# A two-layer decoder on one core: the last turns by VectorE and transfers, and another division of labour in the opening

## The chip, the cores and the metric

One core of a Trainium2 chip. TensorE (PE) does the matrix products; VectorE (DVE), ScalarE (ACT) and GpSimd (POOL) work on tiles in SBUF (on chip, 128 partitions) and PSUM (where TensorE's sums land); SyncE (SP) does nothing but issue transfers, which GpSimd and ScalarE can also issue. Each engine runs its instructions in order. The metric is the device time of one execution in microseconds; the kernel before took 2267.51 us as a median of three runs (2267.19 to 2268.31).

## The reference

A decoder of two layers over 272 tokens (16 learned ones ahead of 256), width 2048, 16 heads of 128. Layer 0 attends with a forget gate, layer 1 by stick-breaking over keys and values that come from the residual stream; each is followed by a squared-ReLU network of width 8192.

```python
for layer in range(2):
    a = rms_norm(h, norm_attn[layer])
    if layer == 0:
        q, k, v, f = split(a @ fox_w_in)               # 2048 x (3*2048 + 16)
        cum = cumsum(log_sigmoid(f + b_f))
        o = forgetting_attention(q, k, v, cum)          # softmax(q k^T * s + cum_q - cum_k) v
        h = h + o @ fox_w_o
    else:
        k, v = split(rms_norm(h, kv_norm) @ w_kv)
        o = stick_breaking_attention(a @ sb_w_q, k, v)
        h = h + o @ sb_w_o
    h = h + square(relu(rms_norm(h, norm_mlp[layer]) @ w_up[layer])) @ w_down[layer]
return rms_norm(h, final_norm)[:, 16:]
```

All inputs and the output are 32-bit floats.

## The kernel before

**Products.** The residual stream lies in `hT` with the width on the partitions: 16 chunks of 128 x 272. Every large product runs in groups (`gemm_group`, one number `u` each, 96 in all): 512 columns of weights, four accumulators `acc`, and for each of four blocks `kb` of four chunks two tiles `raw_u_kb_hf` of 512 KB by SyncE's queue. Weights and x are split in two rounded parts, a high one by ScalarE (`whi`, L210; `x_a` and its like, L125) and the rest by VectorE (`wlo`, L211; L126), and three of the four products of parts are taken (L177). A weight part of a pair of chunks is 128x1024; VectorE reads `raw` and `whi` for it, both in SBUF.

**Order of the engines.** A scheduler places the instructions by their data. Around small work the program pins an instruction behind a numbered product of the running group (`behind(ins, issued[k])`, where `issued` lists the group's 192 products), so that an issue of a transfer or a copy falls at a chosen place. A transfer that is queued waits in its issuing engine's order.

**The opening.** The first group loads x and weights in pieces: the first eight chunks one by one, weights of the first chunk in two halves. Per chunk, ScalarE makes the high part of x, VectorE the rest. `Norm.add` squares each chunk on ScalarE (`sq_a`, L142, two buffers) and adds it to `ssq_a` on VectorE (L143); `finish` sums over partitions by a product with `mean_w` (`pms_a`, L148) and makes `rstd`, which the evictions of the second group need. `load_gates` loads the weights of the forget gate and builds `wf` and `both` (four small instructions of VectorE); 16 products with `hT` give the gate (`pf`, L341).

**Turns.** Attention needs values with tokens on the partitions, while they come with the head's width there. For the first three groups of four heads, VectorE turns 32x32 squares (`squares`, L395), `scratch` writes them to DRAM (`v_dram`, 8 transfers on GpSimd's queue), and `values_back` reads them back as whole turned tiles during the next group of products. For the last group of each layer `token_major` turns on TensorE instead, by products with the identity `ident` into PSUM (`pv`, L381), just ahead of the products `po` (L421, L623, L795) that use them; these run within the first group of the output projection. In layer 1 the corner of the scores is turned on TensorE as well (`pm`, L760), and that of the values (`pvc`, L782) for each of the four groups; in layer 0 by VectorE and transfers (`corner_turned`, `rows_turned`), but for the last group (`pvm`, L606). Near the end `to_token_major` turns the last four chunks of `hT` on TensorE (`ph`, L815) and ScalarE copies them to `h_tok`.

Of the kernel before, what the change touches and what calls it, by code (L numbers as in the profile page):

```python
# [15 lines left out]
P = 128  # L16
D = 2048
NC = D // P
M = 16
# [14 lines left out]
def yoco_kernel(ctx: ExitStack, tc: tile.TileContext, hT_in, gains, b_f, w_f, w_qkv0, w_o0, w_up, w_dn,  # L34
# [87 lines left out]
    def split_chunk(sp, gi, c):  # L122

        g = g_sb[:, gi, c:c + 1]
        nc.scalar.activation(sp.hi[:, c], hT[:, c, sp.t0:], AF.Copy, scale=g)  # L125
        nc.vector.scalar_tensor_tensor(out=sp.lo[:, c], in0=hT[:, c, sp.t0:], scalar=g,  # L126
                                       in1=sp.hi[:, c].bitcast(F32), op0=ALU.mult, op1=ALU.subtract)

    class Norm:


        def __init__(self, label, t0):
            self.label, self.t0 = label, t0
            self.acc = tmp.tile([P, T], F32, tag="ssq", bufs=1, name=f"ssq_{label}")

        def add(self, c):
# [6 lines left out]
            nc.vector.tensor_tensor(out=self.acc[:, t0:], in0=self.acc[:, t0:], in1=sq[:, t0:], op=ALU.add)  # L143
# [42 lines left out]
    def weights(u, kb, wblk, o1, load_x=None):  # L186
# [14 lines left out]
        for hf in range(2):  # L201
# [3 lines left out]
            if load_x is not None and kb == hf == 0:  # L205
                boxes[:1] = [(0, 1, 0, 256), (0, 1, 256, 512)]
# [8 lines left out]
    def gemm_group(wblk, sp, t0, evac, before={}, after={}, load_x=None):  # L215
# [7 lines left out]
        for kb in range(4):  # L223
# [14 lines left out]
            for kcs, ms in runs:  # L238
                pairs = ((0, sp.hi), (0, sp.lo), (1, sp.hi))
                if t0:  # L240
# [5 lines left out]
                wide = [(0, 0, 0), (1, 0, 1), (2, 1, 1)] if t0 and (u % 4 == 1 or u == 91) else []  # L246
                if u == 90:

                    wide = [(0, 0, 0), (0, 0, 1), (0, 2, 1)]
                for kc, m, part, x in products:  # L250
                    first, left[m] = kb == kc == 0 and left[m] == 3 * len(kcs), left[m] - 1
                    nw = n
                    if m == (0 if u == 90 else 3) and x is sp.hi and (kb, kc, part) in wide:
                        x, nw = sp.wide, n + 6
# [40 lines left out]
    norm = Norm("a0", 0)  # L295
    xa = Split("a0", 0)
    box = {}

    def load_x(chunks):
# [4 lines left out]
        for c in chunks:  # L304
            split_chunk(xa, G_A0, c)

    def first_norm(kb):
        if kb == 1:
            box["wf"] = load_gates()
# [11 lines left out]
    def load_gates():  # L321
        nc.scalar.dma_start(bf_sb, b_f)

        wf_sb = att.tile([P, NC, NC], F32, tag="v_sb", name="wf_sb")
        wf = att.tile([P, NC, 2 * NC], F32, tag="v_sb", name="wf")
        nc.scalar.dma_start(wf_sb, w_f)
        nc.vector.memset(wf[:, :, NC:], 0.0)
        nc.vector.tensor_tensor(out=wf[:, :, :NC], in0=wf_sb, in1=g_sb[:, G_A0, :].unsqueeze(2).to_broadcast([P, NC, NC]), op=ALU.mult)
        both = att.tile([P, P], F32, tag="pk", name="both")[:, :32]
        nc.vector.tensor_tensor(out=both, in0=ident[:, :32], in1=ident[:, 32:64], op=ALU.add)  # L330
        for i in (2, 3):
            nc.vector.tensor_tensor(out=both, in0=both, in1=ident[:, 32 * i:32 * i + 32], op=ALU.add)
        both = both[:, :NC]
        return wf, both

    def gate_products():
        wf, _ = box["wf"]
# [6 lines left out]
    def forget_gates(rstd):  # L344
# [4 lines left out]
        nc.tensor.matmul(pf[:NC, :T], box["wf"][1], parts, start=True, stop=True)  # L349
# [26 lines left out]
    def token_major(vT, pr, t0, label):  # L376

        pv = patt.tile([P, 2, 2, P], F32, tag="patt", name=f"pv_{label}")
        for i in range(2):
            for b in range(2):  # L380
                nc.tensor.transpose(pv[:, i, b, :], vT[:, 2 * pr + i, t0 + b * P:t0 + b * P + P], ident)  # L381
        v0 = att.tile([P, 2, 2, P], F32R, tag="v_sb", name=f"v0_{label}")
        v1 = tmp.tile([P, T], F32, tag="u2", name=f"v1_{label}")[:, :2 * P].rearrange("p (i d) -> p i d", i=2)
        split(v0, pv[:, :, 0, :])
        return v0, v1, nc.scalar.copy(v1, pv[:, :, 1, :]).ins

# [18 lines left out]
    def values_back(t, read, use, label):  # L405
        for pr in range(2):
            behind(nc.gpsimd.dma_start(t[:, pr], v_dram[pr].rearrange("c j a x -> (c j) (a x)")), read[pr])
        vs = []
        for pr in range(2):
            v0 = att.tile([P, 2, 2, P], F32R, tag="v_sb", name=f"v0_{label}_{pr}")  # L410
            v1 = tmp.tile([P, T], F32, tag="u2", name=f"v1_{label}_{pr}")[:, :2 * P].rearrange("p (i d) -> p i d", i=2)
            back = t[:, pr].rearrange("p (a b h i) -> p b h a i", a=4, b=2, h=2)
            behind(split(v0.rearrange("p x h (a i) -> p x h a i", a=4), back[:, 0]), use[pr])
            behind(nc.scalar.copy(v1.rearrange("p h (a i) -> p h a i", a=4), back[:, 1]), use[pr])
            vs.append((v0, v1))
        return vs
# [34 lines left out]
    def rows_turned(packs, dst, write, read, label):  # L451
# [5 lines left out]
        for a in range(4):  # L457
            behind(nc.gpsimd.dma_start(m_dram[:n].rearrange("k c j a x -> a j (k c) x")[a],
                                       t[32 * a:32 * a + 32].rearrange("j (m x) -> j m x", x=32)), write)
        behind(nc.gpsimd.dma_start(dst.rearrange("p (k y) -> p k y", k=n), m_dram[:n].rearrange("k c j a x -> (c j) k (a x)")), read)  # L460
# [32 lines left out]
    for g in range(4):  # L493
# [100 lines left out]
        turned = squares(vT, "s", f"0_{g}") if g < 3 else None  # L594
# [8 lines left out]
        if turned is None:  # L603
# [336 lines left out]
```

## Time and profile before

| what | value |
|---|---|
| median of three runs | 2267.51 us (2267.19 to 2268.31) |
| the profiled execution | 2266.66 us |
| its span, first to last instruction | 2264.9 us |
| granted TensorE clock | 1.000 |
| instructions in the span | 44932 |
| mean traffic with DRAM | 191 GB/s |

The span is what the profile covers; some 1.8 us of the execution lie outside it. A row of a timeline gives start and duration in us, the engine, the line, the operation, the tile written and the tiles read, their shapes, and how many instructions the row joins; in brackets stands the time the engine was idle before it and what ended that. Matmuls are pipelined: the duration of one is longer than the distance to the next, so that only distances between starts tell what one costs. An fp32 product is recorded as one or two instructions, depending on its operands.

### The profile page before, as it was taken

The numbers are of one execution on the slowest core, as the hardware profiler recorded it, in microseconds if no ns is written. First come the engines' busy times: TensorE is split into PE (matmuls) and PEld (weight loads), VectorE is DVE, ScalarE is ACT, GpSimd is POOL, SyncE is SP. The second block draws the span as 40 slices with busy tenths as digits, with TensorE's granted clock in tenths as the row PEclk, the third lists the DMA queues.
The fourth block names the chain that finished last, engine by engine and source line by source line (L and its number), as shares of the span: only waits on it lengthen the run. The fifth ranks groups of instructions, "written<-read, shape, count | busy, mean of one in ns | idle before, by whom it ended". The sixth has DMA issues, their size and how long they took to land.

```text
span 2264.9 us, 44932 instructions
## 1 busy us (share of the span) xinstructions
PE 2257.3 (100%) x18816; PEld 2249.7 (99%) x18816; DVE 1347.1 (59%) x1957; ACT 1059.2 (47%) x1444; POOL 105.2 (5%) x201
## 2 busy tenths in 40 slices
PE   9999999999999999999999999999999999999998
PEld 9999999999999999999999999999999999999998
DVE  7777666554455455455566677766555555555555
ACT  6444445443354344344444455555544543543554
POOL 1321210000000000000000011100000000000001
PEclk9999999999999999999999999999999999999999
DMA  7766655555555555555565566666656656566564
GB/s 240 241 199 193 226 184 175 182 172 181 182 173 182 177 175 184 175 184 177 169 192 183 181 215 209 210 208 187 198 187 195 202 189 197 188 193 201 186 200 140
DMA packets 127500, 432.32 MB, mean 191 GB/s; under 512 B 16145, under 2 KB 22817, under 8 KB 127297
## 3 DMA queue, kind: packets, MB, share of 16 engines
q1 hardware_dynamic: 119520, 412.59, 56.8%
q0 software_dynamic: 5456, 13.44, 1.9%
q10 hardware_dynamic: 2320, 3.43, 0.5%
q8 instruction: 147, 2.41, 0.4%
q14 instruction: 57, 0.46, 0.1%
HBM read 417.42 MB, written 11.98 MB: 190 GB/s over the span
## 4 chain that ended last, share of the span: by engine, by line
PE 99%; DMA 0%; ACT 0%; DVE 0%; issue 0%; POOL 0%; POOLq 0%; SPq 0%; ACTq 0%; DVEq 0%
PE acc L177 97%; PE po L421 1%; PE ps L421 0%; PE pz L421 0%; DMA raw<-w_qkv 0%; PE pz L742 0%; PE ps L539 0%; PE po L623 0%; PE po L795 0%; DMA hT<-hT_in 0%; ACT whi L210 0%; PE pf L341 0%; DVE wlo L211 0%; PE pv L381 0%; ACT x_a L125 0%
## 5 line engine op out<-in xcount | busy, mean ns | idle before, releaser
L211 DVE TENSOR_TENSOR wlo<-raw,whi 128x1024 fp32r<-128x1024 f32 (+1 forms) x773 | 928.0, 1216 | 702.7 <-ACT whi L210 695.4
L210 ACT ACTIVATE whi<-raw 128x1024 fp32r<-128x1024 f32 (+1 forms) x773 | 797.3, 1051 | 982.8 <-PE acc L177 946.4
L177 PE MATMUL acc<-x_m,whi 128*128 128x272 f32 (+1 forms) x4096 | 643.0, 281 | 0.0
L177 PE MATMUL acc<-x_u,whi 128*128 128x272 f32 (+1 forms) x3968 | 626.0, 281 | 0.0
L177 PEld LDWEIGHTS acc<-x_m,whi 128*128 128x128 f32 x4096 | 565.8, 188 | 0.1
L177 PEld LDWEIGHTS acc<-x_u,whi 128*128 128x128 f32 x3968 | 550.2, 188 | 0.0
L177 PE MATMUL acc<-x_m,wlo 128*128 128x272 f32 (+1 forms) x2048 | 440.7, 281 | 0.0
L177 PE MATMUL acc<-x_u,wlo 128*128 128x272 f32 (+1 forms) x1984 | 431.5, 281 | 0.0
L177 PE MATMUL acc<-x_a,whi 128*128 128x272 f32 (+1 forms) x2048 | 352.2, 285 | 0.4 <-ACT x_a L125 0.3
L177 PEld LDWEIGHTS acc<-x_m,wlo 128*128 128x128 f32 x2048 | 323.3, 188 | 0.0
L177 PEld LDWEIGHTS acc<-x_u,wlo 128*128 128x128 f32 x1984 | 315.1, 188 | 0.0
L177 PEld LDWEIGHTS acc<-x_a,whi 128*128 128x128 f32 x2048 | 300.0, 188 | 1.9 <-issue 0.9
L177 PE MATMUL acc<-x_a,wlo 128*128 128x272 f32 (+1 forms) x1024 | 252.9, 285 | 0.2 <-DVE wlo L211 0.2
L177 PE MATMUL acc<-x_kv,whi 128*128 128x272 f32 x1024 | 192.8, 288 | 0.0
L177 PEld LDWEIGHTS acc<-x_a,wlo 128*128 128x128 f32 x1024 | 175.5, 188 | 0.8 <-DVE ssq_a L143 0.4
L177 PE MATMUL acc<-x_o,whi 128*128 128x272 f32 (+1 forms) x1024 | 162.5, 282 | 0.0
L177 PEld LDWEIGHTS acc<-x_kv,whi 128*128 128x128 f32 x1024 | 160.2, 188 | 0.0
L177 PE MATMUL acc<-x_kv,wlo 128*128 128x272 f32 x512 | 147.4, 288 | 0.0
L177 PEld LDWEIGHTS acc<-x_o,whi 128*128 128x128 f32 x1024 | 141.8, 188 | 0.0
L292 DVE TENSOR_TENSOR hT<-acc,hT 128x272 f32<-128x272 f32 (+1 forms) x156 | 67.4, 432 | 75.4 <-PE acc L177 75.2
L177 PE MATMUL acc<-x_o,wlo 128*128 128x272 f32 (+1 forms) x512 | 110.4, 281 | 0.0
L177 PEld LDWEIGHTS acc<-x_kv,wlo 128*128 128x128 f32 x512 | 96.5, 188 | 0.0
(227 smaller groups left out, 1107.4 us busy)
## 6 DMA issues: line engine op xcount, KB each, us to landing
raw<-w_up SPq DMA_DIRECT2D x256, 512.0 KB, 4.3
raw<-w_dn SPq DMA_DIRECT2D x256, 512.0 KB, 4.3
raw<-w_qkv SPq DMA_DIRECT2D x92, 512.0 KB, 4.3
raw<-w_o SPq DMA_DIRECT2D x64, 512.0 KB, 4.4
raw<-w_kv SPq DMA_DIRECT2D x64, 512.0 KB, 4.5
raw<-w_q SPq DMA_DIRECT2D x32, 512.0 KB, 4.2
p_dram<-raw_p POOLq DMA_DIRECT2D x32, 96.0 KB, 3.6
raw_p<-p_dram POOLq DMA_DIRECT2D x8, 384.0 KB, 5.0
```

Of the source, the lines that this page charges most:

```text
L177: ins = nc.tensor.matmul(*args, **kw).ins
L210: on_act = nc.scalar.activation(hp, src, AF.Copy)
L211: on_dve = nc.vector.tensor_tensor(out=lp, in0=src, in1=hp.bitcast(F32), op=ALU.subtract)
L292: nc.vector.tensor_tensor(out=hT[:, c, t0:], in0=acc, in1=hT[:, c, t0:], op=ALU.add)
L421: product = nc.tensor.matmul(out, a[i], b[j], start=start and k == 0, stop=stop and k == 2)
```

## The change

It moves 31 of the transposes on TensorE to VectorE and transfers: the values of the last group of heads in both layers, the corner of the scores in layer 1 (all four groups), the corner of the values there (three of four), and the last four chunks of `hT`. The last heads' products (`pair`) are now called from inside the first group of the output projection, behind the products that `places` numbers, and the values' transfers go partly by SyncE's queue. In the opening VectorE makes both parts of chunk 0's x, the weights of chunk 1 are split in halves, the products of chunk 0 go part by part, `wf` and `both` are built at the start, and the 15 adds of the first norm run on GpSimd. Three extra-wide products (262 columns for 256) go, and three others move from group 90 to 61.

```diff
-    def split_chunk(sp, gi, c):
+    def split_chunk(sp, gi, c, on_dve=False):
         g = g_sb[:, gi, c:c + 1]
-        nc.scalar.activation(sp.hi[:, c], hT[:, c, sp.t0:], AF.Copy, scale=g)
+        if on_dve:
+            nc.vector.tensor_scalar(sp.hi[:, c], hT[:, c, sp.t0:], g, None, op0=ALU.mult)
+        else:
+            nc.scalar.activation(sp.hi[:, c], hT[:, c, sp.t0:], AF.Copy, scale=g)
...
-            nc.vector.tensor_tensor(out=self.acc[:, t0:], in0=self.acc[:, t0:], in1=sq[:, t0:], op=ALU.add)
+            self.engine.tensor_tensor(out=self.acc[:, t0:], in0=self.acc[:, t0:], in1=sq[:, t0:], op=ALU.add)
...
-                boxes[:1] = [(0, 1, 0, 256), (0, 1, 256, 512)]
+                boxes = [(o, 1, c, c + 256) for o in range(2) for c in (0, 256)]
...
-                if t0:
+                if t0 or (load_x is not None and kb == 0 and kcs == [0]):
                     products = [(kc, m, *pair) for pair in pairs for kc in kcs for m in ms]
...
-                wide = [(0, 0, 0), (1, 0, 1), (2, 1, 1)] if t0 and (u % 4 == 1 or u == 91) else []
-                if u == 90:
-                    wide = [(0, 0, 0), (0, 0, 1), (0, 2, 1)]
+                wide = [(0, 0, 0), (1, 0, 1), (2, 1, 1)] if t0 and u % 4 == 1 else []
+                if u == 61:
+                    wide = wide + [(3, 0, 0), (3, 0, 1), (3, 2, 1)]
                 for kc, m, part, x in products:
+                    if len(issued) in between:
+                        between[len(issued)]()
...
-    norm = Norm("a0", 0)
+    norm = Norm("a0", 0, nc.gpsimd)
...
+    box["wf"] = gate_tiles()
...
-            split_chunk(xa, G_A0, c)
+            split_chunk(xa, G_A0, c, c == 0)
...
-    def token_major(vT, pr, t0, label):
-        pv = patt.tile([P, 2, 2, P], F32, tag="patt", name=f"pv_{label}")
-        for i in range(2):
-            for b in range(2):
-                nc.tensor.transpose(pv[:, i, b, :], vT[:, 2 * pr + i, t0 + b * P:t0 + b * P + P], ident)
...
-    def scratch(t, products):
+    def scratch(t, products, queues=(nc.gpsimd, nc.gpsimd)):
...
-                ins = nc.gpsimd.dma_start(v_dram[pr].rearrange("c j a x -> a j c x")[a], y[32 * a:32 * a + 32])
+                ins = queues[pr].dma_start(v_dram[pr].rearrange("c j a x -> a j c x")[a], y[32 * a:32 * a + 32])
...
+    def values_read(t, pr, read, queue=nc.gpsimd):
+        behind(queue.dma_start(t[:, pr], v_dram[pr].rearrange("c j a x -> (c j) (a x)")), read)
...
-        turned = squares(vT, "s", f"0_{g}") if g < 3 else None
+        turned = squares(vT, "s", f"0_{g}")
+        if g == 3:
+            scratch(turned, (issued[-20], issued[-1]), (nc.gpsimd, nc.sync))
...
+    def last_heads(turned, reads, uses, places, label, pair, first=None):
+        def back(pr):
+            def run():
+                if first is not None and pr == 0:
+                    box["small"] = first()
+                pair(pr, values_back(turned, pr, issued[uses[pr]], label))
+            return run
+        def read(pr):
+            return lambda: values_read(turned, pr, issued[reads[pr]], nc.sync)
+        return {**{reads[pr] + 1: read(pr) for pr in range(2)}, **{places[pr]: back(pr) for pr in range(2)}}
+
+    box["last"] = last_heads(turned, (32, 60), (70, 108), (96, 122), "0_3", pair)
...
-        pm = patt.tile([P, 512], F32, tag="patt", name=f"pm1_{g}")
-        placed_behind(nc.tensor.transpose(pm[:, 0:P], corners(z[:, :, P:144], z[:, :, 400:416], f"sm1_{g}"), ident), product)
+        pmq = corner_turned(corners(z[:, :, P:144], z[:, :, 400:416], f"sm1_{g}"), f"1_{g}")
...
-        turned = squares(vT, "pp", f"1_{g}") if g < 3 else None
+        turned = squares(vT, "pp", f"1_{g}")
         if g < 3:
             scratch(turned, issued[-2:])
+        else:
+            scratch(turned, (issued[-20], issued[-1]), (nc.gpsimd, nc.sync))
...
+            if g < 3:
+                rows_turned([vc], vc_sb, issued[24], issued[84], f"1_{g}", nc.sync)
             else:
...
+                nc.tensor.transpose(pv[:, :P], vc, ident)
+                nc.scalar.copy(vc_sb, pv[:, :P])
...
+    box["last"] = last_heads(turned, (36, 66), (80, 116), (104, 132), "1_3", pair1, corner1)
...
     def to_token_major():
-        for b in range(2):
-            ph = patt.tile([P, 512], F32, tag="patt", name=f"ph_{b}")
-            for i in range(4):
-                nc.tensor.transpose(ph[:, i * P:(i + 1) * P], hT[:, 12 + i, M + b * P:M + (b + 1) * P], ident)
-            nc.scalar.copy(h_tok[:, b, :], ph)
+        t = squares(hT[:, 12:, M:], "pp", "h")
+        scratch(t, issued[-2:])
+        return t
+
+    def tokens_back(t):
+        for pr in range(2):
+            behind(nc.gpsimd.dma_start(t[:, pr], v_dram[pr].rearrange("c j a x -> (c j) (a x)")), issued[40 + 8 * pr])
+            back = t[:, pr].rearrange("p (a b h i) -> p b h a i", a=4, b=2, h=2)
+            for b in range(2):
+                y = h_tok[:, b, 2 * P * pr:2 * P * pr + 2 * P].rearrange("p (h a i) -> p h a i", h=2, a=4)
+                behind(nc.gpsimd.tensor_copy(y, back[:, b]), issued[80 + 8 * pr])
```

`gate_tiles` holds the allocation of `wf_sb` and `wf`, the memset of `wf` and the three sums of `both` that stood in `load_gates`.

How the instructions move. VectorE in the opening, from the second chunk's weight part to the third block's, before: the weight parts are `wlo`, the x parts `x_a`, and between them stand the norm's adds (`ssq_a`) and the gate's tiles (`wf`, `both`).

```order
L211 TENSOR_TENSOR wlo_1_1_276<-raw_1_1_252,whi_1_1_275 128x512
L327 MEMSET wf 128x16x16
L330 TENSOR_TENSOR both<-ident 128x32
L143 TENSOR_TENSOR ssq_a_138<-ssq_a_138,sq_a_4_291 128x272
L332 TENSOR_TENSOR both<-both,ident 128x32
L143 TENSOR_TENSOR ssq_a_138<-ssq_a_138,sq_a_5_294 128x272
L126 SCALAR_TENSOR_TENSOR x_a_139<-hT,g_sb,x_a_139 128x272
L332 TENSOR_TENSOR both<-both,ident 128x32
L126 SCALAR_TENSOR_TENSOR x_a_139<-hT,g_sb,x_a_139 128x272
L211 TENSOR_TENSOR wlo_2_0_366<-raw_2_0_351,whi_2_0_365 128x2x512
```

The same stretch of VectorE now:

```order
L214 TENSOR_TENSOR wlo_1_1_285<-raw_1_1_261,whi_1_1_284 128x512
L129 SCALAR_TENSOR_TENSOR x_a_139<-hT,g_sb,x_a_139 128x272
L214 TENSOR_TENSOR wlo_1_1_285<-raw_1_1_261,whi_1_1_284 128x512
L129 SCALAR_TENSOR_TENSOR x_a_139<-hT,g_sb,x_a_139 128x272 x2
L214 TENSOR_TENSOR wlo_2_0_368<-raw_2_0_353,whi_2_0_367 128x2x512
```

Nothing but parts is left there; the adds stand one after the other on GpSimd, behind its masks.

TensorE where the norm's sum is taken (`pms_a`), before: it stands among the products of the second accumulator of the second group.

```order
L177 MATMUL acc_1_580<-x_a_139,whi_0_0_587 128x272 x2
L177 MATMUL acc_1_580<-x_a_139,wlo_0_0_588 128x272
L177 MATMUL acc_1_580<-x_a_139,whi_0_1_591 128x272 x2
L177 MATMUL acc_1_580<-x_a_139,wlo_0_1_592 128x272
L148 MATMUL pms_a_536<-ssq_a_138,mean_w 128x272
```

And now:

```order
L180 MATMUL acc_3_165<-x_a_139,wlo_3_1_454 128x272
L347 MATMUL pf<-hT,wf 32x272 x3
L180 MATMUL acc_0_581<-x_a_139,whi_0_0_589 128x272 x2
L151 MATMUL pms_a_538<-ssq_a_138,mean_w 128x272
L180 MATMUL acc_0_581<-x_a_139,wlo_0_0_590 128x272
```

It has moved up to behind the group's second product (it was behind the 22nd), and three of the last four gate products stand right before that group.

SyncE at the hand-over from the last heads of layer 0 to the output projection, now (`w_o` are the projection's weights); before, the weight transfers followed each other with nothing between:

```order
L202 DMA raw_2_1_4208<-w_o 128x1024
L202 DMA raw_3_0_4301<-w_o 128x1024
L397 DMA v_dram_157<-turned_3_4050 32x4x128 x4
L202 DMA raw_3_1_4302<-w_o 128x1024
L401 DMA turned_3_4050<-v_dram_156 128x512
L401 DMA turned_3_4050<-v_dram_157 128x512
L202 DMA raw_0_0_4387<-w_o 128x1024
```

The second pair's four writes and both reads now stand between weight transfers; the first pair's writes go by GpSimd's queue.

More of the change, by code (lines that the diff above doesn't have):

```diff
@@ L628, in yoco_kernel, with pair @@
-        if g == 3:
-            outputs()
-    def out_proj(w, ao, t0, gi, label, before={}):
+        def pair(pr, v, g=g, pps=pps, own=own):
+            p0, p1 = in_order(*pps[pr])
+            v0, v1 = v
+            po = patt.tile([P, 2, 256], F32, tag="patt", name=f"po0_{g}_{pr}")
+            for i in range(2):
+                weighted(po, v0, p0, i)
+                nc.tensor.matmul(po[:, i, P:], v1[:, i, :], p1[:, i], start=False, stop=i == 1)
+            ends = po.rearrange("p i (c q) -> p (i c) q", c=2)[:, :, P - M:]
+            nc.vector.tensor_tensor(out=ends, in0=ends, in1=own[:, 4 * pr:4 * pr + 4], op=ALU.add)
+            put_split(ao, 4 * g + 2 * pr, 2, M, S, po)
@@ new lines, in outputs @@
+        def outputs(g=g, pps=pps, turned=turned, vm=vm, vc=vc, vm_sb=vm_sb, small_outputs=small_outputs, pair=pair):
+            behind(split_probabilities(*pps[1]), issued[60])
+            scratch(turned, issued[20:60:20])
+            for pr in range(2):
+                values_read(turned, pr, issued[100 + 10 * pr])
+            vs = [values_back(turned, pr, issued[160 + 10 * pr], f"0_{g}") for pr in range(2)]
+            rows_turned([vm, vc], vm_sb, issued[112], issued[130], f"0_{g}")
+            small_outputs()
+            for pr in range(2):
+                pair(pr, vs[pr])
```

152 lines of the change are left out of this document (66 added, 86 removed).

## The prediction

> **What bounds the kernel now.** I read the page's busy times first, then the chain of waits, then the waits of TensorE alone.
>
> ```profile
> PE 2257.3 (100%) x18816; PEld 2249.7 (99%) x18816; DVE 1347.1 (59%) x1957; ACT 1059.2 (47%) x1444; POOL 105.2 (5%) x201
> PE 99%; DMA 0%; ACT 0%; DVE 0%; issue 0%; POOL 0%; POOLq 0%; SPq 0%; ACTq 0%; DVEq 0%
> PE pr_fin L177 <- DVE fin L852: 0.8, 1, 0.8
> PE acc L177 <- ACT x_a L125: 0.3, 1, 0.3
> PE acc L177 <- DVE wlo L211: 0.2, 1, 0.2
> ```
>
> TensorE (PE) is busy for 2257.3 of the span of 2264.9 us, the chain is PE for 99%, and once it has begun it waits for 1.3 us in all (the columns are total, times, longest), of which the change touches the last two rows, 0.5 us. So there are two ways to move the end: take work off TensorE (the turns), or change how well the opening feeds it. VectorE (DVE, 59%) and ScalarE (ACT, 47%) have room as a mean over the span; the opening is where they have none.
>
> **The turns.** 31 transposes leave TensorE: 16 into `pv`, 8 into `ph`, 4 into `pm`, 3 of 4 into `pvc`. The timeline of TensorE shows each kind beside its neighbours (start, duration):
>
> ```profile
> 2101.52 1.04 PE L815 MATMUL ph<-ident,hT 128*128 128x128 f32 x8
> 2102.31 0.83 PE L177 MATMUL acc<-x_m,whi 128*128 128x262 f32 x5
> ...
> 321.87 0.60 PE L381 MATMUL pv<-ident,vT 128*128 128x128 f32 x4
> 322.23 0.49 PE L177 MATMUL acc<-x_o,whi 128*128 128x272 f32 x2
> ...
> 325.51 0.38 PE L381 MATMUL pv<-ident,vT 128*128 128x128 f32 x2
> 325.65 0.37 PE L421 MATMUL po<-p,v 128*128 128x256 f32 x1
> 325.85 0.38 PE L381 MATMUL pv<-ident,vT 128*128 128x128 f32 x2
> ...
> 1471.67 1.03 PE L381 MATMUL pv<-ident,vT 128*128 128x128 f32 x8
> 1472.57 0.60 PE L177 MATMUL acc<-x_o,whi 128*128 128x256 f32 x3
> ...
> 1307.34 0.27 PE L760 MATMUL pm<-ident,pk_sm 128*128 128x128 f32 x1
> 1307.37 0.49 PE L177 MATMUL acc<-x_kv,whi 128*128 128x272 f32 x2
> ...
> L381 PE MATMUL pv<-ident,vT x16: 271/272/273, 321.9 to 1472.4; 128*128 128x128 f32 x16
> ```
>
> A transpose lasts 0.272 us, but the next instruction starts long before it ends, so what it costs is the distance to that start. `ph`: 2102.31 - 2101.52 = 0.79 us for 8. `pv` in layer 0: 0.36 for 4, then 0.14 for 2, twice. In layer 1: 0.90 for 8 with the one `pvc` behind them. A lone `pm`: 0.03; four of them and two `pvc` more, 0.18. Together 0.79 + 0.36 + 0.28 + 0.90 + 0.18 = 2.5 us, the low end. The products beside them gain too: the lone `po` at 325.65 holds 0.20 us where its neighbours of the same shape need some 0.12. The high end is 31 times the pitch of a whole product, 31 x 0.12 = 3.7. I take **-3.2**, since most transposes stand in blocks with a change of operand at both ends. The block of gate products is split once more, one such change: **+0.1**. The three extra-wide products fewer have 6 columns each; nothing.
>
> [...]
>
> What takes the turns over has no one waiting: SyncE only issues, VectorE has 41% of its time idle, and the last turn's values (`h_tok`) are wanted some 150 us later. The exception is the last group of heads in each layer, where `pv` was turned on the spot and now goes to DRAM and back.
>
> ```profile
> 314.00 0.44 DVE L503 TENSOR_TENSOR vT<-acc,rstd_a 128x272 f32<-128x272 f32 x1 [1.04 <-PE acc L177]
> 317.07 0.33 SPq L199 DMA_DIRECT2D raw<-w_o  x1
> v_dram<-turned POOLq DMA_DIRECT2D x48, 64.0 KB, 3.8
> turned<-v_dram POOLq DMA_DIRECT2D x12, 256.0 KB, 5.3
> raw_p<-p_dram SPq DMA_DIRECT2D x8, 384.0 KB, 3.4
> ```
>
> The last of the four value tiles is there at 314.44. Behind it VectorE has a weight part of 1.2 us and the turns of the second pair, so SyncE can write these from about 316.5, in four issues of some 0.4 us; then comes the weight transfer that was at 317.07 (now near 318.2), then the read of the first pair at 318.6. That pair is turned two evictions, some 3 us, earlier; GpSimd writes it from 313, four issues of 0.55 and 3.8 to landing, 319.0. The read takes 3.4 to 5.3, ScalarE's and VectorE's halves 0.9: 323.3 to 325.2. The first `po` stands two products ahead of 325.51, at 325.3, less the 0.36 of the `pv` before it, 324.9: between 1.6 us of cover and a stall of 0.3. The second pair lands at 318.1 + 3.8, is read after it and ready at 326.2 to 328.1, and its `po` comes some 3 us after the first. Layer 1 has the same order of steps. I take **+0.3** for both layers, bounds 0 and 2 x 1.9 (a read by the slower row where I count on the faster one). Behind the reads on SyncE wait the next weights, 1 to 3 us later than before; a stall there is not in the sum and belongs to the fourth rival.
>
> **The opening.** Taking chunk 0's x to VectorE and chunk 1's weights in halves can save only what TensorE idles there:
>
> ```profile
> 6.55 0.41 PE L177 MATMUL acc<-x_a,wlo 128*128 128x272 f32 x2
> 7.04 1.27 PE L177 MATMUL acc<-x_a,whi 128*128 128x272 f32 x8
> 6.35 0.63 ACT L210 ACTIVATE whi<-raw 128x512 fp32r<-128x512 f32 x1 [0.38 <-DMA raw<-w_qkv]
> 4.26 0.42 ACT L210 ACTIVATE whi<-raw 128x256 fp32r<-128x256 f32 x1 [2.17 <-DMA raw<-w_qkv]
> ```
>
> Two products of 0.12 end at 6.80, the next start at 7.04, bound by the split of 512 columns that starts at 6.35 when its weights land. With 256 columns (0.42 instead of 0.63) it is there 0.2 earlier: **-0.2**. An earlier start of the first product (0.3 waited) is worth no more, since that landing comes next.
>
> The adds of the first norm are the part that can go wrong. The trace has no 128x272 add on GpSimd (POOL), but it has adds and copies of GpSimd beside VectorE:
>
> ```profile
> 2250.75 1.62 POOL L839 TENSOR_TENSOR ob<-h_tok,g_tok 128x256 f32<-128x256 f32 x2 [170.46 <-DVE h_tok L838]
> 2250.97 0.80 DVE L844 CUSTOM_DVE_ANT_0 sq_tok<-h_tok 128x256 f32<-128x256 f32 x1
> ...
> 40.31 0.29 POOL L432 COPY pk_qm<-qT 128x128 f32<-128x128 f32 x1 [34.05 <-DVE qT L499]
> ...
> 186.28 2.29 POOL L432 COPY pk_qm<-qT 128x128 f32<-128x128 f32 x1 [9.69 <-DVE qT L499]
> 186.06 2.35 DVE L211 TENSOR_TENSOR wlo<-raw,whi 128x1024 fp32r<-128x1024 f32 x2
> ...
> L432 POOL COPY pk_vm<-vT 128x128 f32<-128x128 f32 x4 | 4.4, 1088 | 3.9 <-DVE vT L503 3.9
> L874 POOL TENSOR_TENSOR ob<-hT,pr_sb 128x256 f32<-128x256 f32 x4 | 2.9, 735 | 4.3 <-ACT pr_sb L870 4.3
> ```
>
> The same copy takes 0.29 us alone and 2.29 when two weight parts of VectorE run back to back over it (mean 1088 ns in the group beside them). The other way round, VectorE's 128x256 operation of 2250.97 ends at 2251.77, and GpSimd's second add, which ends at 2252.37, fits in the 0.60 us after it. [...]
>
> ```profile
> 10.10 0.99 DVE L143 TENSOR_TENSOR ssq_a<-ssq_a,sq_a 128x272 f32<-128x272 f32 x2
> ...
> 15.50 0.27 DVE L327 MEMSET wf<- 128x256 f32 x1
> 16.63 0.49 DVE L126 SCALAR_TENSOR_TENSOR x_a<-hT,g_sb,x_a 128x272 fp32r<-128x272 f32 x1
> 17.56 1.22 DVE L211 TENSOR_TENSOR wlo<-raw,whi 128x1024 fp32r<-128x1024 f32 x1
> ...
> 18.83 0.39 PE L177 MATMUL acc<-x_a,wlo 128*128 128x272 f32 x1 [0.17 <-DVE wlo L211]
> 34.17 0.41 PE L177 MATMUL acc<-x_a,whi 128*128 128x272 f32 x2
> 34.91 0.62 PE L148 MATMUL pms_a<-ssq_a,mean_w 128*128 128x272 f32 x2
> ```
>
> Ahead of the weight part of 17.56, for which TensorE waits at 18.83, VectorE loses two adds (0.99), one more by the same row (0.4), and at 15.50 to 16.63 the memset, sums and two adds (1.13): 2.5 us. Against it stand up to five turns of GpSimd of 0.60 x 272/256 = 0.64 us: 3.2. Net **+0.7** there. If GpSimd took nothing from VectorE, the wait itself would go, 0.2 us in the table: the low end is -0.2. The ten later adds cost 10 x (0.64 - 0.36) = 2.8 more if nothing covers them, which is the high end; I count none of it, as VectorE is busy for 59% of the span and makes up a delay once the x is split.
>
> The norm's sum (`pms_a`) is the second place. It stood behind 22 products of the second group and now behind 2: six products take 34.91 - 34.17 = 0.74, so TensorE reaches it 20 x 0.123 = 2.5 earlier, at 32.4, or 32.9 with the +0.7 and -0.2. GpSimd's add alone is 735 ns x 272/256 = 0.78; with the mean wait of the copy (1.09 - 0.29 = 0.80) it is 1.58, and 15 of them from 10.1 end at 33.8: a stall of 0.9, none when the last ones run with VectorE idle. I take **+0.6**. The squares of ScalarE have two buffers, so a late add holds ScalarE too, and the weight parts behind the square.
>
> **The sum**: -3.2 + 0.1 + 0.3 - 0.2 + 0.7 + 0.6 = -1.7 us. The profiled execution took 2266.66 us, its span 2264.9; the median of the runs is 2267.51, 0.85 above. The span should come to 2263.2, and the median to **2265.8**.
>
> **Rivals.**
> A transpose costs its duration (0.11): 31 x 0.272 = 8.4 instead of 3.2 gives -6.9, 2260.6. Against it stand all the rows above in which the next product starts after 0.03 to 0.10 us; for it, that the changes of operand are seen at few places. [...]
> GpSimd takes nothing that counts (0.27): the turns, -0.2 and -0.2 at the waits, 2267.51 - 3.2 + 0.1 - 0.4 = 2264.0. For it: the lone 0.29; against it: the copies of 1 to 2 us.
> GpSimd's chain comes late (0.13, the other side): when each add waits as the copy of 186.28 did, 15 x 2.29 from 10.1 ends at 44.5, 11.6 us after TensorE is at `pms_a`: -2.3 + 11.6 = +9.3, 2276.8. It decides for slower than 0.2% once the stall passes 6.8 us, an add of (32.9 + 6.8 - 10.1) / 15 = 1.97 us; the mean row stands at 1.58.
> The values of the last heads come late in both layers (0.05): 2 x 1.9 in place of 0.3, 2269.3. For it: the waits in order on SyncE; against it: SyncE's own reads of 3.4.
>
> **How the numbers follow.** My forecast has 0.44, its own range 2264.1 to 2268.3. What a measurement of this kernel can tell from no change is about 0.2%, 4.5 us: below 2263.0 or above 2272.0. Faster: the first rival (0.11), a fifth of the second (0.06) and 0.01 of mine, 0.18. Slower: 0.11 of the third, 0.02 of the fourth, 0.01 of mine, 0.14. The rest, 0.68, lies within. The range 2262.4 to 2271.0 leaves out most of the first and of the third rival.
>
> **What would show it.** Right: no transposes of `ph`, `pm`, `pv` on TensorE and some 3 us less between unmoved places on either side of each; GpSimd's adds of more than 1 us while weight parts run; a wait of TensorE on `wlo` near 19 us and one on `ssq_a` near 33. Wrong: adds of 0.8 us with weight parts still at 1.22, or a wait on `v` near 325 and 1478, or ScalarE's squares idle for `sq_a` for several us in a row.

## The result

The changed kernel took 2271.11 us (median of 20 runs, 2267.31 to 2274.4), the kernel before 2267.98 in as many (2266.97 to 2270.19): a ratio of 1.0014 (95% interval 1.0008 to 1.0020), slower by some 3 us. It also spreads more, 7.1 us against 3.2. The profiled execution took 2272.27 us, its span 2270.6.

Of the page after, the busy times and the chain:

```profile
PE 2258.0 (99%) x18785; PEld 2249.5 (99%) x18785; DVE 1356.1 (60%) x1975; ACT 1057.1 (47%) x1439; POOL 132.0 (6%) x246
PE 96%; DMA 2%; DVE 1%; issue 1%; ACT 0%; SPq 0%; POOL 0%; POOLq 0%; ACTq 0%; DVEq 0%
```

TensorE has 31 instructions fewer and is busy for 0.7 us more: what left it came back as slower instructions (below), and the chain now holds 2% of transfers. Its waits after (total, times, longest):

```profile
PE po L414 <- ACT v L378: 3.1, 1, 3.1
PE pvc L806 <- DMA vc_sb<-m_dram: 1.9, 2, 1.5
PE idle L61 <- DVE mean_w L57: 1.1, 1, 1.1
PE pr_fin L180 <- DVE fin L881: 0.8, 1, 0.8
```

The first two are new, and both belong to turned values of layer 1. The other two stood there before, with the same 1.1 and 0.8 us. How the difference builds up is seen from the first product of each group in the two traces (start in the changed kernel less start in the kernel before; then the difference of two such numbers over a stretch):

| stretch | difference, us |
|---|---|
| opening, to the second group | +1.29 |
| layer 0's hand-over, first group of its projection | -0.88 |
| layer 1's keys and values | +1.62 |
| layer 1's hand-over, first group of its projection | +4.14 |
| the turn of `hT` near the end, two groups | -0.92 |
| everything else, up to the last group's first product | +0.0 |
| behind it, to the end of the span | +0.4 |

Of the last row, 0.3 us show as well in the run below that has nothing of the change but the adds on GpSimd, so the row is not put down to the turns.

Layer 1's hand-over on SyncE's queue after (start, duration, what is issued):

```profile
1472.77 0.34 SPq L473 DMA_DIRECT2D raw_p<-p_dram  x1
1473.21 0.66 SPq L202 DMA_DIRECT2D raw<-w_o  x1
1474.06 2.32 SPq L397 DMA_DIRECT2D v_dram<-turned  x4
1476.42 0.46 SPq L202 DMA_DIRECT2D raw<-w_o  x1
1479.48 0.83 SPq L401 DMA_DIRECT2D turned<-v_dram  x2
```

and the engines around it, GpSimd, ScalarE and TensorE:

```profile
1469.25 2.20 POOL L397 DMA_DIRECT2D v_dram<-turned  x4 [0.49 <-DVE turned L390]
1483.33 0.42 ACT L378 ACTIVATE v<-turned 128x256 fp32r<-128x256 f32 x1 [3.53 <-DMA turned<-v_dram]
1483.80 0.51 PE L414 MATMUL po<-p,v 128*128 128x256 f32 x2 [3.10 <-ACT v L378]
```

GpSimd had issued the first pair's writes by 1471.45, and they had landed by 1474.8. Their read, the second in the last row, goes out at 1479.99: ahead of it on SyncE stand the read of the probabilities (which waits for its own write), a weight transfer, the second pair's four writes, another weight transfer, and the second pair's read, which the scheduler put first and which waits until those four writes have landed. TensorE stands still from 1480.7 to 1483.8.

That is 3.1 of the 5.0 us lost there (4.14, and some 0.9 that the eight transposes had cost by the rows before). The windows of TensorE behind the wait show the rest (busy, granted clock, share and rate of the transfers):

```profile
1483.80:1485.00 1.20, 1.20 (x11) 1.00 0.87 236
1485.00:1486.00 1.00, 1.00 (x9) 0.63 0.86 332
1486.00:1487.00 1.00, 1.00 (x6) 0.50 0.89 356
1487.00:1488.00 1.00, 1.00 (x7) 0.50 0.88 307
1488.00:1489.00 1.00, 1.00 (x8) 0.67 0.93 320
1489.00:1490.00 1.00, 1.00 (x11) 1.00 0.58 234
```

The granted clock is half for 0.74 + 1 + 1 + 0.66 = 3.4 us (a window's shortfall from 1.00, divided by 0.5), which costs 1.7 us of products; it sets in 1.5 us after TensorE is busy again.

The corners of the values in layer 1, third group, on SyncE's queue, and the product on TensorE that uses them:

```profile
1422.05 2.20 SPq L451 DMA_DIRECT2D m_dram<-vt  x4
1424.35 0.39 SPq L202 DMA_DIRECT2D raw<-w_kv  x1
1430.49 0.34 SPq L453 DMA_DIRECT2D vc_sb<-m_dram  x1
1433.84 0.46 PE L806 MATMUL pvc<-pm_sb,vc_sb 128*128 128x128 f32 x2 [1.54 <-DMA vc_sb<-m_dram]
```

The last write is issued by 1424.25; the read goes out 6.2 us later, when all four have landed, and TensorE waits 1.54 us for what it brings.

### The profile page after: what moved, and what is told of

Read it like the earlier page. It is cut to its first block, busy times and chain, and to the rows that moved or that the text cites. A ratio compares the mean times of both kernels' runs of the same rounds, so it can differ in the third digit from the quotient of the medians.

```text
span 2270.6 us, 45002 instructions
## 1 busy us (share of the span) xinstructions
PE 2258.0 (99%) x18785; PEld 2249.5 (99%) x18785; DVE 1356.1 (60%) x1975; ACT 1057.1 (47%) x1439; POOL 132.0 (6%) x246
## 4 chain that ended last, share of the span: by engine, by line
PE 96%; DMA 2%; DVE 1%; issue 1%; ACT 0%; SPq 0%; POOL 0%; POOLq 0%; ACTq 0%; DVEq 0%
PE acc L180 94%; DMA m_dram<-vt 1%; PE po L414 0%; DMA vc_sb<-m_dram 0%; PE ps L414 0%; PE pz L414 0%; DMA raw<-w_qkv 0%; DVE wlo L214 0%; ACT whi L213 0%; PE pz L753 0%; PE ps L532 0%; PE po L808 0%; PE po L611 0%; DMA v_dram<-turned 0%; DMA turned<-v_dram 0%
## 5 line engine op out<-in xcount | busy, mean ns | idle before, releaser
L180 PE MATMUL acc<-x_o,wlo 128*128 128x272 f32 (+2 forms) x512 | 111.7, 284 | 0.0
```

What stands on the lines that cost most here:

```text
L180: ins = nc.tensor.matmul(*args, **kw).ins
```

## The experiments

Each time is the median of its runs, with its ratio to the kernel before on the same chip. The stretches are taken from the one profile of each run, as in the table above.

**The order of the two reads.** Only in layer 1 does it change anything: there the second pair's read is now pinned behind the first's.

```diff
-        behind(queue.dma_start(t[:, pr], v_dram[pr]...), read)
+        ins = queue.dma_start(t[:, pr], v_dram[pr]...)
+        behind(ins, read)
+        if pr and "read0" in box:
+            behind(ins, box.pop("read0").ins)
...
```

> The changed kernel with one thing altered: on SyncE the read of the first pair's turned values goes ahead of the read of the second pair's in layer 1 (in the changed kernel it stands behind it, and the second pair's read waits for the second pair's writes to land). Theory A, the order on SyncE's queue makes the 3.1 us wait of TensorE ahead of po in layer 1: the wait falls below 0.5 us, the granted clock stays at 1.00 after it, the stretch from the first to the second group of layer 1's output projection goes from 4.1 us longer than in the kernel before to about 1 us shorter, and the whole comes to about 2266 (ratio to before 0.999 to 1.000). Rival B, the transfers are simply that slow and the order does not matter: a wait of 2.5 us or more stays and the ratio stays near 1.0014.

2269.93 us, ratio 1.0007 (0.9999 to 1.0016). SyncE and TensorE:

```profile
1477.35 2.29 SPq L401 DMA_DIRECT2D turned<-v_dram  x2
1482.63 0.50 PE L418 MATMUL po<-p,v 128*128 128x256 f32 x2 [2.02 <-ACT v L378]
```

The first pair's read goes out at 1477.35 instead of 1479.99, but the wait only falls to 2.0: this read took 4.8 us to land instead of 3.3, and TensorE comes to `po` three products earlier. The clock stayed at 1.00, and the stretch is at +1.65. Neither theory holds as it stands, and one profile settles little: where the hand-over is not edited and `po` stands where it does in the changed kernel, the wait is 3.1, 2.7, 2.4 and 0.8 us in the profiles of this set. From the group's first product to the landing of the first pair's values it is 13.6 us here, and with the order of the changed kernel 14.4 to 15.1 in six profiles and 12.7 in a seventh (the next run). So the order seems to be a part of it, of about 1 us.

**The corners on GpSimd's queue.**

```diff
-                rows_turned([vc], vc_sb, issued[24], issued[84], f"1_{g}", nc.sync)
+                rows_turned([vc], vc_sb, issued[24], issued[84], f"1_{g}")
```

> The changed kernel with the transfers of the turned corner of the values in layer 1 (m_dram, vc_sb, first three groups) on GpSimd's queue instead of SyncE's. Theory A, these transfers wait in SyncE's queue among 512 KB weight transfers: the two waits of TensorE on vc_sb (0.4 and 1.5 us) go, the stretch of layer 1's key and value groups goes from 1.7 us longer than before to about 0.3 shorter, and the total falls by some 2 us (ratio about 1.0005). Rival B, turning by transfers takes that long on any queue: waits of over 1 us in sum stay.

2267.88 us, ratio 1.0003 (0.9993 to 1.0012). The waits on `vc_sb` are gone, and layer 1's keys and values take 0.80 us less than in the kernel before. With the corners on SyncE this stretch was +1.62, +1.28, +0.60, +0.51, -0.20 and between -0.66 and -0.82 in the profiles of the other runs here: the transfers are late in some executions and not in others, one source of the wider spread.

The outcome is theory A's, but its reason is not shown. The corners are no sooner back by GpSimd's queue: from the last write's issue to the read's it is 4.3 to 5.8 us there (three groups) and 3.8 to 6.6 on SyncE's (nine profiles), and in the third group the corner lands at 1435.57 here and at 1433.70 in the changed kernel. What moved is the product that waits for it: it stands behind the 178th product of its group instead of the 144th, at 1437.44 instead of 1433.84. The scheduler placed it anew with the other queue. Corners on SyncE with the later place were not run.

Nor is the lower total the corners' alone. In this profile the hand-over, which was not edited, lost less too (+1.28):

```profile
PE po L414 <- ACT v L378: 0.8, 1, 0.8
```

Here SyncE reads the probabilities back 2.7 us after the group's first product instead of 4.5, and all behind it on the queue goes out earlier.

**The norm's adds back on VectorE.**

```diff
-    norm = Norm("a0", 0, nc.gpsimd)
+    norm = Norm("a0", 0)
```

> The changed kernel with the 15 adds of the first norm back on VectorE; the rest of the new opening stays. Theory A, GpSimd and VectorE take turns at SBUF and the adds on GpSimd hold VectorE's weight and x parts: VectorE's x parts after 11 us take 0.49 again instead of up to 1.0, the second group starts about 0.4 us earlier than in the kernel before instead of 1.25 later, total lower by 1.5 us (ratio about 1.0007). Rival B, the opening's loss comes from the chunk-by-part order and the splits in halves: the second group still starts 1.0 us or more later than before.

2269.28 us, ratio 1.0006 (0.9997 to 1.0014); the profile is of the slowest run, 2271.89. The second group starts 0.10 us before that of the kernel before, instead of 1.25 after it. The groups of the opening in the changed kernel, on GpSimd and then VectorE (count, then busy us and mean ns):

```profile
L146 POOL TENSOR_TENSOR ssq_a<-ssq_a,sq_a 128x272 f32<-128x272 f32 x15 | 16.6, 1107 | 10.7 <-ACT sq_a L145 10.0
```

```profile
L214 DVE TENSOR_TENSOR wlo<-raw,whi 128x1024 fp32r<-128x1024 f32 x7 | 10.6, 1541 | 0.6 <-ACT whi L213 0.6
L129 DVE SCALAR_TENSOR_TENSOR x_a<-hT,g_sb,x_a 128x272 fp32r<-128x272 f32 x13 | 9.7, 771 | 0.7 <-ACT x_a L128 0.7
```

The same two groups of VectorE in the kernel before:

```profile
L211 DVE TENSOR_TENSOR wlo<-raw,whi 128x1024 fp32r<-128x1024 f32 x7 | 8.4, 1218 | 0.5 <-ACT whi L210 0.5
L126 DVE SCALAR_TENSOR_TENSOR x_a<-hT,g_sb,x_a 128x272 fp32r<-128x272 f32 x14 | 6.8, 495 | 0.0
```

Beside GpSimd's adds (1107 ns against 440 on VectorE) a weight part takes 1541 ns instead of 1218 and an x part 771 instead of 495. That the two engines take turns at SBUF, as theory A has it, no run shows.

**The adds on GpSimd alone**, in the kernel before, and **the old opening** in the changed kernel:

```diff
-            nc.vector.tensor_tensor(out=self.acc[:, t0:], in0=self.acc[:, t0:], in1=sq[:, t0:], op=ALU.add)
+            self.engine.tensor_tensor(out=self.acc[:, t0:], in0=self.acc[:, t0:], in1=sq[:, t0:], op=ALU.add)
```

```diff
-    norm = Norm("a0", 0, nc.gpsimd)
+    norm = Norm("a0", 0)
...
-            split_chunk(xa, G_A0, c, c == 0)
+            split_chunk(xa, G_A0, c)
...
-                boxes = [(o, 1, c, c + 256) for o in range(2) for c in (0, 256)]
+                boxes[:1] = [(0, 1, 0, 256), (0, 1, 256, 512)]
...
-                if t0 or (load_x is not None and kb == 0 and kcs == [0]):
+                if t0:
```

> The kernel before with one part of the change: the 15 adds of the first norm on GpSimd, nothing else. Theory A, GpSimd and VectorE take turns at SBUF: the second group starts 1.0 to 2.0 us later than in the kernel before, GpSimd's adds take over 1 us on average, VectorE's x parts beside them up to 1.0 instead of 0.49 (ratio 1.0005 to 1.0009). Rival B, GpSimd's adds cost VectorE nothing and free it of 15 adds: the second group starts at the same time or up to 0.4 earlier (ratio 0.9998 to 1.0000).

> The changed kernel with the old opening (adds on VectorE, chunk 0's x by ScalarE, chunk 1's weights whole, products of chunk 0 in the old order; the gate's tiles are still built at the start); the turns stay changed. Theory A, of the opening only the adds on GpSimd cost anything and the rest brings nothing: the second group starts within 0.4 us of the kernel before, as with the adds alone put back. Rival B, the other parts of the new opening cost or gain more than 0.5 us of their own. The hand-over of layer 1 and its corners keep their waits, so the ratio is near 1.0006 in both cases; the segments tell.

The adds alone: 2269.6 us, ratio 1.0010 (1.0001 to 1.0019), the second group 2.1 us later, and another 0.5 up to the sixth group. The old opening: 2268.92, ratio 1.0005 (0.9996 to 1.0014), the second group 0.22 later. So far both follow theory A: the adds cost, the rest of the new opening is worth nothing that shows. Over the whole set, from the thirteenth product to the second group TensorE needs 25.1, 25.2, 25.6 and 26.0 us where VectorE adds, 25.3 in the kernel before, and 25.9 to 27.0 (eight profiles) in the changed opening with GpSimd: 1.1 us more in the mean.

Most of that is not the slower parts, which is all that theory A names. With the adds on GpSimd (nine profiles) the last four gate products stand on TensorE in two blocks, one and three; with the adds on VectorE (five profiles, the kernel before among them) they stand in one. The block before with the product behind it, and the two blocks of the changed kernel:

```profile
26.66 0.67 PE L341 MATMUL pf<-hT,wf 128*32 128x272 f32 x8
27.26 0.40 PE L177 MATMUL acc<-x_a,wlo 128*128 128x272 f32 x1
```

```profile
27.25 0.65 PE L347 MATMUL pf<-hT,wf 128*32 128x272 f32 x2
27.83 0.39 PE L180 MATMUL acc<-x_a,wlo 128*128 128x272 f32 x1
32.98 0.66 PE L347 MATMUL pf<-hT,wf 128*32 128x272 f32 x6
33.57 0.52 PE L180 MATMUL acc<-x_a,whi 128*128 128x272 f32 x2
```

From the first gate product to the product behind the block it is 0.60 us for four of them, 0.58 for one and 0.59 for three (two records each): the block has a price, its length hardly. The second block costs 0.7 us in the changed kernel, 0.75 in the mean of the eight. That leaves some 0.3 us in the mean for the slower parts; in the profile of the changed kernel they cost TensorE nothing, in the run with the adds alone 1.2.

**Layer 1's last heads**, three ways: the first pair's products 16 products later (the second pair's 4); the first pair's read on GpSimd's queue; the turn by TensorE, as before.

```diff
-    box["last"] = last_heads(turned, (36, 66), (80, 116), (104, 132), "1_3", pair1, corner1)
+    box["last"] = last_heads(turned, (36, 66), (80, 116), (120, 136), "1_3", pair1, corner1)
```

```diff
-            return lambda: values_read(turned, pr, issued[reads[pr]], nc.sync)
+            return lambda: values_read(turned, pr, issued[reads[pr]], queues[pr])
...
-    box["last"] = last_heads(turned, (36, 66), (80, 116), (104, 132), "1_3", pair1, corner1)
+    box["last"] = last_heads(turned, (36, 66), (80, 116), (104, 132), "1_3", pair1, corner1, (nc.gpsimd, nc.sync))
```

```diff
-        turned = squares(vT, "pp", f"1_{g}")
+        turned = squares(vT, "pp", f"1_{g}") if g < 3 else None
...
-    xm, norm_m = out_proj(w_o1, ao, M, G_M1, "m1", box.pop("last"))
+    xm, norm_m = out_proj(w_o1, ao, M, G_M1, "m1", {}, {1: tensor1})
```

(`tensor1` calls `token_major` for both pairs and `pair1` on what it returns.)

> The changed kernel with the last heads' products of layer 1 placed 16 products later (120 and 136 instead of 104 and 132). Theory A, the granted clock falls to half only after a wait of TensorE of some 3 us: the wait shrinks by 16 x 0.113 = 1.8 to about 1.3 us and the slow stretch of 3 us goes with it, so the stretch to the next group gains 1.8 and some 2.3 more, 4 us in all (ratio about 0.9997). Rival B, the clock falls after any wait there, or for another reason: 1.8 us gained, and the clock still shows 0.5 for about 3 us (ratio about 1.0006).

> The changed kernel with the read of the first pair's turned values in layer 1 on GpSimd's queue, where nothing stands behind the first pair's writes; SyncE keeps the second pair. Theory A, the wait ahead of po comes from what stands before this read on SyncE (the second pair's writes, a weight transfer, the second pair's read): the read is issued near 1475.7 by the span of the changed kernel instead of 1480.0, and even with GpSimd's slower landing of some 5 us the wait falls from 3.1 to below 1.0 us, with no slow clock behind it; ratio about 1.0000. Rival B, the traffic of weights at this place makes any read late: wait of 2 us or more.

> The changed kernel with the last heads of layer 1 turned by TensorE as in the kernel before; everything else stays changed. Theory A, this hand-over alone is where the change loses its gain: the stretch to the projection's second group takes the time it takes in the kernel before (within 0.3 us) instead of 4.1 more, and the total falls by some 3 to 4 us below the changed kernel's (ratio 0.9997 to 1.0002), with less spread among runs. Rival B, the loss is spread over other places: the ratio stays above 1.0008.

Later products: 2273.16 us, ratio 1.0022 (1.0012 to 1.0033), where theory A had 0.9997; against the changed kernel's 1.0014 (1.0008 to 1.0020) the difference is not clear of the intervals. The profile is of the fastest run (2270.00). In it the wait on the values is 1.3 as expected and the clock stays at 1.00, but two new waits stand behind it:

```profile
PE po L414 <- ACT v L378: 1.3, 1, 1.3
PE acc L180 <- DVE x_o L458: 1.2, 1, 1.2
PE pvc L806 <- ACT vc_sb L794: 1.1, 1, 1.1
```

The projection needs these heads' outputs (`x_o`) in its last block, and their halves on ScalarE and VectorE no longer fit ahead of it. Neither of the two places is free: at the earlier one the values come too late for the products, at the later one the products come too late for the projection. The read on GpSimd's queue: 2267.8, ratio 1.0001 (0.9992 to 1.0010); no wait on values is left (they land 11.3 us after the group's first product), the stretch is at +1.05, all of it a wait of 1.3 us on `x_o`. Theory A holds here. The turn by TensorE: 2267.27, ratio 1.0000 (0.9991 to 1.0009), the stretch at +0.03, and the runs lie within 1.9 us. Theory A of the last: the hand-over of layer 1 alone accounts for some 3 us of the median.

**The clock.** The first products of these heads 16 products earlier and ahead of all that follows, so that the wait grows; and the same with 36 products of a constant ahead of them.

```diff
-    box["last"] = last_heads(turned, (36, 66), (80, 116), (104, 132), "1_3", pair1, corner1)
+    box["last"] = last_heads(turned, (36, 66), (80, 116), (88, 132), "1_3", pair1, corner1)
```

```diff
+            if pr == 0 and g == 3:
+                filler = patt.tile([P, 512], F32, tag="patt", name="filler")
+                for _ in range(36):
+                    nc.tensor.matmul(filler[:, :P], mean_w, mean_w, start=True, stop=True)
```

> The changed kernel with the last heads' first products of layer 1 put 16 products earlier and ahead of all that follows, so that TensorE's wait there grows to some 5 us. Theory A, a wait of TensorE longer than about 3 us halves the granted clock for a while after it: windows behind the wait show 0.50 for about 3 us. Rival B, the slow stretch in the changed kernel came from something else (traffic, the instructions there): no slow clock, or one that also shows without a wait. Total near or above the changed kernel's (ratio 1.0015 to 1.0025).

> The same as the run with the earlier place, but TensorE fills the wait with 36 products of a constant (some 4.2 us). Theory A: the values come at the same time, the wait that is left is under 2 us, the clock stays at 1.00 behind it, and the next group starts 1.5 to 2.5 us earlier than without the filler. Rival B: the clock shows 0.50 here too, and the next group starts no earlier.

Bare: 2274.28 us, ratio 1.0030 (1.0018 to 1.0042); filled: 2276.34, ratio 1.0037 (1.0023 to 1.0051). The windows of TensorE in the bare run:

```profile
1480.00:1482.00 2.00, 0.00 (x0) 0.58 0.87 274
1482.00:1484.00 2.00, 1.33 (x6) 0.50 0.89 283
1484.00:1485.00 1.00, 1.00 (x7) 0.50 0.94 377
1485.00:1486.00 1.00, 1.00 (x6) 0.50 0.74 283
1486.00:1487.00 1.00, 1.00 (x7) 0.50 0.88 240
1487.00:1488.00 1.00, 1.00 (x10) 0.93 0.34 113
```

in the filled one:

```profile
1484.00:1485.00 1.00, 1.00 (x12) 1.00 0.92 348
1485.00:1486.00 1.00, 1.00 (x11) 1.00 0.81 324
1486.00:1487.00 1.00, 1.00 (x11) 1.00 0.40 164
```

and the filler's row in its timeline (36 products, two records each):

```profile
1476.70 8.20 PE L806 MATMUL filler<-mean_w 128*128 128x128 f32 x72
```

With a wait of 5.0 us the clock is half for 1.7 + 2 + 3 + 0.1 = 6.8 us, from 1480.3 on, while TensorE still waits; with the wait filled it is never below 1.00 there. That is theory A as to the clock. The filler was mis-sized: one such product holds 0.22 us, not 0.12, so it ran 2.9 us past the values and the next group started 1.9 us later, not earlier.

Half clock came with the waits of 2.7 us (3.4 us of it, in the run with the old opening), 3.1 us (3.4, in the changed kernel) and 5.0 us (6.8, in the bare run). Behind waits of 1.3 us (the later products), 1.5 (the third corner in the changed kernel), 2.0 (the order of the reads) and 2.4 (the adds on VectorE) the clock stayed at 1.00. The 2.7 is less than the some 3 us of theory A. Whether the length of a wait alone decides is not shown, as a single profile stands for each of these.

**The repairs together**: corners on GpSimd's queue and adds on VectorE, with layer 1's last heads either read on GpSimd's queue or turned by TensorE (the edits above).

> Three repairs at once: the first pair's read in layer 1 on GpSimd's queue, the turned corner of the values in layer 1 on GpSimd's queue, the first norm's adds on VectorE. If the losses are these three and add up, by segments against the kernel before: opening -0.1, layer 0's hand-over -0.9, layer 1's corners -0.7, its hand-over between -0.9 and 0, the end -0.9; in sum -2.6 to -3.5 us, ratio 0.9985 to 0.9989. Rival: the transfers on GpSimd's queue collide, and the waits come back under other names; ratio above 0.9995.

> The repairs with layer 1's last heads turned by TensorE as before, its corners of the values on GpSimd's queue, and the adds on VectorE. If the segments add up: opening 0 to +0.6, layer 0 -0.9, layer 1's corners -0.7, its hand-over 0, the end -0.9: -1.9 to -2.5 us, ratio 0.9989 to 0.9992, with waits of TensorE on values or corners gone. Rival: ratio above 0.9996.

By GpSimd's queue 2265.44 us, ratio 0.9990 (0.9981 to 0.9999), just short of what was expected, the opening at +0.8 instead of -0.1; by TensorE 2264.65, ratio 0.9984 (0.9976 to 0.9993), better than expected. Both are faster than either kernel. One at a time, corners, adds and the turn by TensorE lowered the ratio from 1.0014 by 0.0011, 0.0008 and 0.0014, 0.0033 in sum; together they lower it by 0.0030. So by the medians, too, these three places hold the loss, each figure to about 0.001. In the second no wait is left but those of the kernel before at both ends:

```profile
PE idle L61 <- DVE mean_w L57: 1.1, 1, 1.1
PE pr_fin L180 <- DVE fin L900: 0.8, 1, 0.8
```

Its stretches: opening +0.3, layer 0 -0.88, layer 1's keys and values -0.80, its hand-over +0.03, the end -0.92; with 0.4 up to the sixth group some -2 us in the profile, as expected.

## Why the prediction was wrong, step by step

- **The turns, -3.2: right.** Where nothing waited for what took their place, 23 transposes gave 0.88 + 0.80 + 0.92 = 2.6 us, and the eight of layer 1's last heads stood for some 0.9 more by the rows before, 3.5 together. The distance between starts was the price (2.6 us for 23, 0.11 each), not the duration (0.272); the rival by the duration falls.
- **The hand-over, "Layer 1 has the same order of steps. I take +0.3 for both layers": the step that failed.** Layer 0 went as worked out (no wait, -0.88). Layer 1 has another order: SyncE also carries the probabilities there, whose read waits for its write, and the scheduler had put the second pair's read first. It cost 5.0 us in the profile where 0.15 was counted: 3.1 of waiting and 1.7 of half clock, which the prediction did not know of. With the turn back on TensorE the loss is gone (+0.03), and with the first pair's read off SyncE no wait on values is left. How the 3.1 divide between the probabilities and the order of the two reads is not settled. The fourth rival had this mechanism with a price of 3.8 for two layers and a chance of 0.05.
- **"What takes the turns over has no one waiting": wrong for the corners of the values in layer 1.** Their four writes and the read on SyncE were given no price; they cost up to 2.4 us in a profile (+1.62 against -0.80). The product that uses them stands too early for such a round trip; that the queue is to blame is not shown.
- **The opening, -0.2 + 0.7 + 0.6 = +1.1: near in size by luck**, 1.29 in the profile and 1.1 to 1.7 in the eight with this opening. VectorE's parts are slower beside GpSimd's adds (1541 ns for 1218, 771 for 495). The +0.7 counts five turns of GpSimd of 0.64 us against VectorE, and no run shows such turns: in their place the runs show the slower parts, which cost TensorE some 0.3 us in the mean. In the profile, 0.7 us is the split block of gate products, for which the sum has **+0.1**, and another 0.7 the first nine products, which stand some 0.23 us apart instead of 0.12. They end at 7.28 us. What slows them is not shown; how many are so slow varies from run to run (one in the kernel before, at 5.14). TensorE did not wait for `ssq_a` (+0.6), nor longer for the weight part near 19 us than before (+0.7); and with the first products at full pace the pause of the -0.2 was still there (0.42 us between two products near 7 us, with the adds on VectorE).

By the profile it is -3.5 for the turns, +1.3 for the opening, +5.0 for the hand-over and +2.4 for the corners, +5.2 in sum; the groups' starts differ by 5.25 at the end. The median lies at +3.1, as the waits of layer 1 vary.

## What to carry to other kernels

A turn that goes through DRAM must be followed instruction by instruction through the queue that issues it, in each place where it is used: here the first pair's values lay in DRAM at 1474.8 and their read went out at 1479.99, behind all that stood ahead of it on SyncE, where the second pair's read alone held the queue from 1476.88 to 1479.48, until its writes had landed. Where TensorE is the bound, a wait of 3.1 us cost 4.8 here, because the clock fell to half behind it for 3.4 us; it did so behind one of 2.7 too, and not behind four of 1.3 to 2.4. Before a repair is put down to a queue, look whether the product that waited still stands in its old place. Adds moved to GpSimd were not free (1107 ns each instead of 440, and VectorE's weight parts beside them 1541 instead of 1218), and products on TensorE moved with them: the last four gate products, split into two blocks, were paid twice (0.58 and 0.59 us, for 0.60 in one block).

## What was not expected

Besides the clock: in two profiles (adds on VectorE; the filled wait) TensorE's 256-column products have a pitch of 118 ns instead of 113 for some 70 us after layer 1's hand-over, at a granted clock of 1.00, 2.7 us in all; a row of eight in the filled run and one in the changed kernel:

```profile
1520.99 1.11 PE L180 MATMUL acc<-x_o,whi 128*128 128x256 f32 x8
```

```profile
1520.94 1.07 PE L180 MATMUL acc<-x_o,whi 128*128 128x256 f32 x8
```

In both it sets in behind a wait in the first group of the projection and ends at the first extra-wide product of the fourth group after it (`u` 65); the three groups between have none. In the changed kernel, too, products stand 118 ns apart just ahead of an extra-wide one of the first group (the 145th product), and 113 behind it. So in all three places the longer pitch ends at one of these products, which the change moves about; what brings it on stays open, as other runs wait at the same place without it.
